# Seven block products for eight in the last two column chunks of a feed-forward input projection

## The chip, the cores and the metric

The kernel runs on one core of a Trainium2 chip. The metric is the device time of one execution in microseconds (us), the median of several. Five engines work side by side, each through its own list of instructions in order: TensorE (PE) multiplies, VectorE (DVE), ScalarE (ACT) and GpSimd (POOL) do elementwise work, SyncE (SP) issues the DMA transfers. Semaphores tie them together.

## The reference

Two layers of a decoder trunk on 256 tokens of width 1024, in float32: a feed-forward block, a mixer (gated DeltaNet and a causal convolution, merged by gates), and a second feed-forward block. There are four feed-forward blocks in all:

```python
def swiglu_ffn(h, w_in, w_out):
    gate, up = jnp.split(h @ w_in, 2, axis=-1)
    return (jax.nn.silu(gate) * up) @ w_out
...
    f = swiglu_ffn(rmsnorm(x, ffn1_norm_pre[i]), ffn1_w_in[i], ffn1_w_out[i])
    x = x + 0.5 * rmsnorm(f, ffn1_norm_post[i])
```

`w_in` is 1024 x 5632, `w_out` 2816 x 1024. The kernel scales by the norm's factor after the product, at the gate.

## The kernel before

**Numbers.** Every float32 operand is split in two: a high part, which ACT makes by a cast to PE's float32 form (`whi`, `xt[:, 0]`), and a low part, the rest, which DVE or POOL makes by a subtraction (`wlo`, `xt[:, 1]`). One product is then three matmuls (`mm3`, lines 588 to 591): high by high, high by low, low by high.

**Feed-forward stage** (`ffn`, line 694 on). The input projection (`proj_in`) goes through 11 column chunks of 512 columns (256 of the gate, 256 of the up part). A chunk has four weight tiles of 128 x 1024 (512 KB), each two 128-row pieces of the inner dimension. For both blocks of 128 tokens (`tb` 0 and 1) a weight tile serves 2 x 3 matmuls of 128 x 512, so 12 in all, and a chunk is 48 matmuls for each token block. In the last three stages the first two chunks are done for token block 0 first, while token block 1 is still being normalized. A chunk and token block fill one PSUM bank of four (`ps_mm`, tag `mm`). `ev` gates it: ACT takes Silu of one half, DVE multiplies the other (`ag`). `fin` turns the result by DVE transposes and a round trip through device memory (`way`), and splits it into high and low parts (`act`), the low part on POOL. The output projection (`proj_out`) then goes through 22 weight tiles; its four accumulators (two token blocks, two column halves) are again four `mm` banks. It takes two tiles for token block 0, both halves, then the same two for token block 1.

**Weights.** `Stream` loads the weight tiles in the order of use. A tile arrives in one of four buffers (`raw`), is cast into one of eight `whi` tiles and subtracted into one of eight `wlo` tiles (the ring, `RING = 8`). A `raw` buffer is free when its low part is made, a ring tile when PE has used it. When PE is done with a tile, the next one's load, cast and subtraction are put into the program, and a list scheduler that knows the instructions' dependencies and priorities places them in the engines' queues; PE's order is the written one. Only in the mixers are they put off by a count of matmul groups (`lanes`, `DELAY`, `in_step`), and DVE's and POOL's orders kept as written (`in_order`), with ACT's instructions held behind PE's.

## Time and profile before

| | |
|---|---|
| median of 3 runs | 1352.1 us (1351.65 to 1353.6) |
| profiled execution, span from first to last instruction | 1349.7 us |
| busy, PE / DVE / ACT / POOL | 1327.1 / 933.8 / 732.3 / 445.5 us |
| high-low products of the input projections and mixers, 128 x 512 | 2048 and 1024 matmuls |
| same, output projections | 704 and 352 |
| DMA | 273.76 MB, mean 203 GB/s |

The profiled execution's own time is told by its span only; the median of the runs lies 2.4 us above it, 0.2%. A row such as `L144 PE MATMUL mm<-whi,xt ... x2048 | 647.6, 391` reads: line 144 issued 2048 matmuls that wrote `mm` from `whi` and `xt`, busy for 647.6 us together, 391 ns from start to end of one. Matmuls overlap, so their pace is read from the starts in the timeline. The number after the second bar is the idle time ahead of the group on its engine, and what ended it.

### The profile page before, as it was taken

Reading aid. Unit: us, or ns where it says so; the run is one execution under the profiler, and the core shown is the slowest. Engines: PE = TensorE matmul, PEld = TensorE weight load, DVE = VectorE, ACT = ScalarE, POOL = GpSimd, SP = SyncE. Lnnn points to the kernel's source line nnn. Section 1 sums busy time; section 2 is a strip of 40 time slices with the busy share of each in tenths; the row PEclk is TensorE's granted clock in tenths of the full one; section 3 lists DMA queues with packets and bytes.
Section 4 is the critical chain, followed back from the end, with each engine's and each line's share of the span. In section 5 each row is a group of like instructions: output and inputs, shape, how many; then the busy total and the mean of one; then the engine's idle time right before and its main releaser. Section 6 shows DMA issues by size and latency. Waiting matters only on the chain.

```text
span 1349.7 us, 20220 instructions
## 1 busy us (share of the span) xinstructions
PE 1327.1 (98%) x7259; PEld 1128.0 (84%) x7259; DVE 933.8 (69%) x1594; ACT 732.3 (54%) x1175; POOL 445.5 (33%) x374
## 2 busy tenths in 40 slices
PE   9999999999999999999999999999999999999998
PEld 7888889997787888888888888899977878888886
DVE  6676455999966776665576654579999666766553
ACT  7545447675555545544455543577656564555541
POOL 0111017798744201111011120277986431011110
PEclk9999999999999999999999999999999999999999
DMA  8878746562634666776468775465545446477861
GB/s 274 287 239 260 249 156 210 166 211 96 206 110 153 225 218 222 276 249 221 155 219 280 265 235 186 146 231 172 173 138 183 143 139 234 154 261 247 273 212 39
DMA packets 115652, 273.76 MB, mean 203 GB/s; under 512 B 24768, under 2 KB 48352, under 8 KB 115552
## 3 DMA queue, kind: packets, MB, share of 16 engines
q1 hardware_dynamic: 115264, 272.40, 61.5%
q8 instruction: 57, 0.93, 0.3%
q14 instruction: 43, 0.35, 0.1%
q10 hardware_dynamic: 288, 0.07, 0.0%
HBM read 256.68 MB, written 15.75 MB: 202 GB/s over the span
## 4 chain that ended last, share of the span: by engine, by line
PE 81%; DVE 11%; ACT 3%; DMA 2%; issue 1%; POOL 1%; DVEq 0%; POOLq 0%; SPq 0%; ACTq 0%
PE mm L144 75%; DVE cacc L124 4%; PE gd L144 3%; DVE c L124 3%; DVE wlo L124 2%; PE tr L150 2%; DMA raw<-mw 2%; ACT whi L171 1%; DVE at L124 1%; ACT dt L171 1%; ACT sg L171 0%; DMA raw<-w2i 0%; DVE ssk L124 0%; DVE qk L124 0%; POOL rk L124 0%
## 5 line engine op out<-in xcount | busy, mean ns | idle before, releaser
L144 PE MATMUL mm<-whi,xt 128*128 128x512 f32 (+1 forms) x2048 | 647.6, 391 | 3.0 <-ACT qT L171 2.2
L171 ACT CAST whi<-raw 128x1024 fp32r<-128x1024 f32 (+2 forms) x448 | 458.8, 1035 | 316.8 <-PE mm L144 173.8
L124 DVE TENSOR_TENSOR wlo<-raw,whi 128x1024 fp32r<-128x1024 f32 (+2 forms) x342 | 427.2, 1264 | 190.0 <-ACT whi L171 183.5
L144 PEld LDWEIGHTS mm<-whi,xt 128*128 128x128 f32 x2048 | 382.3, 188 | 82.3 <-ACT qT L171 3.0
L144 PE MATMUL mm<-wlo,xt 128*128 128x512 f32 (+1 forms) x1024 | 396.4, 387 | 0.1
L124 POOL TENSOR_TENSOR wlo<-raw,whi 128x1024 fp32r<-128x1024 f32 (+1 forms) x106 | 250.5, 2379 | 142.5 <-ACT whi L171 140.0
L144 PEld LDWEIGHTS mm<-wlo,xt 128*128 128x128 f32 x1024 | 192.6, 188 | 37.6 <-DVE wlo L124 1.3
L144 PE MATMUL mm<-whi,act 128*128 128x512 f32 x704 | 218.3, 390 | 0.0
L124 POOL TENSOR_TENSOR act<-way,act 128x512 fp32r<-128x512 f32 x44 | 79.1, 1798 | 396.1 <-ACT act L171 385.9
L124 DVE SCALAR_TENSOR_TENSOR cacc<-hT,pc,cacc 128x254 f32<-128x254 f32 (+28 forms) x464 | 179.5, 472 | 0.2
L144 PE MATMUL mm<-xt,whi 128*128 128x256 f32 x960 | 175.5, 285 | 0.8 <-ACT qT L171 0.6
L144 PEld LDWEIGHTS mm<-whi,act 128*128 128x128 f32 x704 | 132.2, 188 | 27.4
L144 PEld LDWEIGHTS mm<-xt,whi 128*128 128x128 f32 x960 | 149.4, 192 | 1.9 <-ACT qT L171 0.9
L144 PE MATMUL mm<-wlo,act 128*128 128x512 f32 x352 | 137.0, 389 | 0.0
L144 PE MATMUL mm<-xt,wlo 128*128 128x256 f32 x480 | 135.9, 283 | 0.0
L171 ACT ACTIVATE ag<-mm,rstd 128x256 f32<-128x256 f32 x88 | 41.7, 474 | 100.0 <-PE mm L144 80.5
L144 PEld LDWEIGHTS mm<-xt,wlo 128*128 128x128 f32 x480 | 92.0, 192 | 0.0
L124 DVE SCALAR_TENSOR_TENSOR ag<-mm,rstd,ag 128x256 f32<-128x256 f32 x88 | 42.3, 481 | 58.7 <-ACT ag L171 58.4
L144 PEld LDWEIGHTS mm<-wlo,act 128*128 128x128 f32 x352 | 66.1, 188 | 13.6
L124 POOL TENSOR_TENSOR rpost<-ss,exp 128x1 f32<-128x1 f32 x12 | 6.5, 538 | 193.8 <-DVE ss L124 193.8
L171 ACT ACTIVATE jk<-mm 128x512 f32<-128x512 f32 x24 | 14.3, 598 | 60.4 <-PE mm L144 60.4
L124 DVE SCALAR_TENSOR_TENSOR c<-mm,pc,c 128x255 f32<-128x255 f32 (+2 forms) x108 | 43.7, 478 | 2.6 <-ACT c L171 2.6
(187 smaller groups left out, 1148.3 us busy)
## 6 DMA issues: line engine op xcount, KB each, us to landing
raw<-mw SPq DMA_DIRECT2D x168, 512.0 KB, 3.8
raw<-w2i SPq DMA_DIRECT2D x88, 512.0 KB, 4.8
raw<-w1i SPq DMA_DIRECT2D x84, 512.0 KB, 4.9
raw<-w1o SPq DMA_DIRECT2D x44, 512.0 KB, 4.7
raw<-w2o SPq DMA_DIRECT2D x44, 512.0 KB, 4.3
way<-way SPq DMA_DIRECT2D x176, 64.0 KB, 1.8
way<-way SPq DMA_DIRECT2D x44, 256.0 KB, 4.8
wbc<-feat SPq DMA_DIRECT2D x13, 512.0 KB, 4.9
```

Of the source, the lines that this page charges most:

```text
L124: r = op(out, *a, **k)
L144: r = self.eng.matmul(o, w, x, **k)
L150: r = self.eng.transpose(*a)
L171: r = op(*a, **k)
```

## The change

Chunks 9 and 10 of every feed-forward input projection (`UNITS = 4*((9,),)`) become one unit. Write X for the activations in 2 x 2 blocks (token block, half of the inner dimension) and W for the two chunks' weights in 2 x 2 blocks (half of the inner dimension, chunk). Instead of eight block products (two token blocks by two chunks by two halves of the inner dimension) there are seven, with four sums of X blocks and four of W blocks as operands, by Winograd's form of Strassen's scheme: `11`, `t1` = 12 - 11, `t2` = 22 - `t1`, `21`, `t3` = `t2` - 11, `22`, `t4` = 21 - `t2`. Each product is 12 matmuls: two weight tiles, each used by six matmuls.

- The X sums (`early`) are made on DVE near the stage's start, split by ACT and DVE, and stay in SBUF.
- The weight blocks 11 and 21 of the unit are kept in slots of their own (`held`), 12 and 22 use the `raw` buffers. DVE makes `t1`, `t2`, `t4` in PSUM banks (`sum`), `t3` in place of block 11; each in two halves of 512 columns. They are then split as other weights are.
- The seven products fill three PSUM banks, here q, r and s. q collects products 1, 3, 5 and 7, with copies taken between (`s1`, `s2`), r products 2 and 6 (copy `s5`), s product 4. Three of the four gates first add such a copy; the last one, after product 7, gates q as it stands.
- From the stage's start to the end of the input projection the loads, casts, sums and low parts of all weights, 120 tiles ahead, are put into the program by a planner (`plan`, `bring`, `best`, `issue`, `pump`): it keeps clocks for PE, DVE, ACT and POOL, and takes on each engine the job that can start first, by due time. DVE, POOL and ACT keep that written order (`in_order`, now on ACT as well). Leaving it (`plan(None)`) first forces the jobs of every tile that the ring holds, and then `lanes.flush()` the steps that are left, the last gate's product among them.
- The gates are steps with a delay (`"gate": (0, 1)`); the activations' low parts move from POOL to DVE; chunks 0 and 1, and 9 and 10, take the `way` round trip together; the numbers of `DELAY["ffn"]` change.

```diff
+UNITS = 4*((9,),)
+
+FORMS = ("11", "t1", "t2", "21", "t3", "22", "t4")
+
+SUMS = {"t1": ("12", "11"), "t2": ("22", "t1"), "t3": ("t2", "11"), "t4": ("21", "t2")}
+
+NEEDS = {"t1": (), "t2": (("t1", "low"),), "t3": (("t2", "summed"), ("11", "low")), "t4": (("t2", "low"), ("t3", "summed"))}
+
+USERS = {"12": (("t1", "summed"),), "22": (("22", "low"), ("t2", "summed")), "11": (("t3", "low"),), "21": (("21", "low"), ("t4", "summed"))}
...
     def __init__(self, eng, pe):
-        self.eng, self.pe, self.tc = eng, pe, None
+        self.eng, self.pe, self.tc, self.at = eng, pe, None, 0.0
+        self.chain, self.before = False, None
+
+    def in_order(self, tc):
+        self.tc, self.chain, self.before = tc, tc is not None, None
...
+                ins = getattr(r, "ins", r)
+                if self.chain:
+                    if self.before is not None:
+                        behind(self.tc, ins, self.before)
+                    self.before = ins
+                behind(self.tc, ins, self.pe.last)
...
+def unit_pieces(src, key, new):
+
+    raws = {(b, j): Raw(src(int(b[0]) - 1, int(b[1]) - 1, j), key(b, j)) for b in ("11", "12", "22", "21") for j in range(2)}
+    ps = {}
+    for j in range(2):
+        banks = Banks(lambda k, j=j: new(j and k))
+        at = {"t1": banks, "t2": banks, "t4": banks, "t3": raws["11", j]}
+        p = {f: Piece(at[f] if f in at else raws[f, j], f, 1.36) for f in FORMS}
+        for f in FORMS:
+            ps[f, j] = p[f]
+            p[f].group = list(raws.values())
+            if f in SUMS:
+                p[f].ins = [banks if b[0] == "t" else raws[b, j] for b in SUMS[f]]
+                p[f].needs = [(p[g], did) for g, did in NEEDS[f]]
+                p[f].parts = [slice(0, 512), slice(512, D)]
+        for b, users in USERS.items():
+            raws[b, j].users = [(p[f], did) for f, did in users]
+    return [ps[f, j] for f in FORMS for j in range(2)]
...
+    def plan(self, lanes):
+        if lanes is not None:
+            self.planned, self.lanes, lanes.stream, self.begun = True, lanes, self, self.pe.at
+            self.raws = []
+            for p in self.pieces[self.nload:self.nload + 120]:
+                for raw in p.group:
+                    if raw not in self.raws:
+                        raw.first = p.n
+                        self.raws.append(raw)
+            self.out = []
+        else:
+            for p in self.pieces[self.taken:self.nload]:
+                self.force(p)
+            self.planned, self.lanes.stream, self.lanes = False, None, None
...
+    def bring(self, now):
+        while self.raws:
+            raw = self.raws[0]
+            self.out = [r for r in self.out if not r.free(now)]
+            if raw.first > self.taken + RING + CFG["far"]:
+                break
+            if sum(r.key == raw.key for r in self.out) >= (4 if raw.key is None else 1):
+                break
+            if self.fetch > now + CFG["depth"]:
+                break
+            self.raws.pop(0)
+            raw.tile = self.fresh() if raw.key is None else self.held(raw.key)
+            self.nc.sync.dma_start(raw.tile[:, :raw.src.shape[-1]], raw.src)
+            self.fetch = max(self.fetch, now) + 1.9
+            raw.landed = self.fetch + CFG["land"]
+            self.out.append(raw)
...
+    def issue(self, eng, t, p, kind):
+        eng.at = t
+        if self.shared(p, kind):
+            self.lock = t + (2.25 if eng is self.gp else 1.08)
+        n = D if p.form else p.raw.src.shape[-1]
+        for c in p.parts if p.form else [slice(0, n)]:
+            if kind == "sum":
+                a, b = (r.part(c) for r in p.ins)
+                with prio(self.tc, "w"):
+                    eng.tensor_tensor(p.raw.part(c), a, b, op=ALU.subtract)
+            elif kind == "high":
+                self.to_high(p, c)
+            else:
+                self.to_low(p, c, eng)
+        setattr(p, {"sum": "summed"}.get(kind, kind), eng.at)
...
+    def force(self, p):
+        until = self.pe.at
+        while p.low is None:
+            until += 0.5
+            if until > self.pe.at + 100:
+                raise RuntimeError(f"stuck {p.n} {p.form}")
+            self.bring(until)
+            self.pump(until)
...
+        if first and early:
+            early()
         for c in range(len(chunks)):
+            if c in units:
+                unit(c)
+            if c in units or c - 1 in units:
+                continue
+            if c == 1 and not first and early:
+                lanes.finish(due[1])
+                early()
...
         def ev(c, tb, ps):
-            a = tokt("ag", [P, 2, 256])
-            S.activation(a[:, 0, :], ps[:, 0:256], AF.Silu, scale=xt[tb][1])
-            V.scalar_tensor_tensor(a[:, 1, :], ps[:, 256:512], xt[tb][1], a[:, 0, :], op0=ALU.mult, op1=ALU.mult)
-            gated[c, tb] = a
-
-
-
-        def fin(c):
-            act.append(slot(c, [P, 2, 2, 2, P], F32R, name="act"))
 
             def steps():
-                way = slot(11 + c % 4, [P, 2, 512], name="way")
-                out4 = way[:, 0].rearrange("p (j k b t) -> p k b j t", j=4, k=2, b=2)
-                for tb in range(2):
-                    a = gated.pop((c, tb))
-                    with prio(tc, "turn"):
-                        V.transpose(out4[:, :, tb], a[:, 1, :].rearrange("p (k j c) -> p k j c", k=2, j=4))
-                turned = dram.tile([4, 32, 4, P], F32, name=f"way{l}{c}")
+                a = gated[c, tb] = tokt("ag", [P, 2, 256])
+                with prio(tc, "ev"):
+                    S.activation(a[:, 0, :], ps[:, 0:256], AF.Silu, scale=xt[tb][1])
+                yield
+                with prio(tc, "ev"):
+                    V.scalar_tensor_tensor(a[:, 1, :], ps[:, 256:512], xt[tb][1], a[:, 0, :], op0=ALU.mult, op1=ALU.mult)
+            job = lanes.add("gate", steps())
+            if st.planned:
+                lanes.step(job)
+            else:
+                lanes.finish(job)
...
+        def fin(*cs):
+            for c in cs:
+                act[c] = slot(c, [P, 2, 2, 2, P], F32R, name="act")
+
+            def steps():
...
+                        S.copy(hi, src)
+                        V.tensor_tensor(lo, src, hi.bitcast(F32), op=ALU.subtract)
...
+            def steps():
+                p21, p11, p12 = ps_tr(), ps_tr(), ps_tr()
+                whole(p21, 1, 0)
+                whole(a[:, 0], 1, 1)
+                V.tensor_tensor(a[:, 1], p21, a[:, 0], op=ALU.add)
+                high(1, a[:, 1])
+                yield
+                whole(p11, 0, 0)
+                V.tensor_tensor(b[:, 0], a[:, 1], p11, op=ALU.subtract)
+                high(2, b[:, 0])
+                low(1, a[:, 1])
+                yield
+                V.tensor_tensor(b[:, 1], a[:, 0], b[:, 0], op=ALU.subtract)
+                high(3, b[:, 1])
+                low(2, b[:, 0])
+                yield
+                whole(p12, 0, 1)
+                V.tensor_tensor(a[:, 0], p12, b[:, 0], op=ALU.subtract)
+                high(4, a[:, 0])
+                low(3, b[:, 1])
+                yield
+                low(4, a[:, 0])
...
+        def unit(c):
+            lanes.finish(sums["job"])
+
+            def product(ps, f, start):
+                for j in range(2):
+                    w = st.peek(0)
+                    for k in range(2):
+                        kt = 2 * j + k
+                        ks = slice(512 * k, 512 * k + 512)
+                        mm3(ps, f[:, 0, kt, :], f[:, 1, kt, :], w[0][:, ks], w[1][:, ks], start and kt == 0, kt == 3,
+                            skip_group_check=True)
+                        lanes.tick()
+                    st.done()
...
+            q, r = ps_mm(), ps_mm()
+            s1, s5 = (work.tile([P, 512], F32, name="sm", tag=f"state{i}", bufs=1) for i in range(2))
+            s2 = slot(14, [P, 512], name="s2")
+            product(q, blk[0, 0], True)
+            kept(q, s1)
+            product(r, sums[1], True)
+            kept(r, s5)
+            product(q, sums[2], False)
+            kept(q, s2)
+            s = ps_mm()
+            product(s, blk[0, 1], True)
+            gate(c, 0, s, s1)
+            product(q, sums[3], False)
+            gate(c + 1, 1, q, s5)
+            product(r, sums[4], False)
+            gate(c + 1, 0, r, s2)
+            product(q, blk[1, 1], False)
+            gate(c, 1, q)
+            fin(c, c + 1)
...
+        proj_in(xt, [(512, 2)] * 11, ev, fin_one, first, units=units, unit=unit, early=early)
+        st.plan(None)
+        lanes.flush()
+        for eng in (V, W, S):
+            eng.in_order(None)
```

What this makes of the engines' lists, at three places of the first stage; the other three have the same rows with other numbers.

DVE, around the last gates of the input projection. Before (`ag_1229` and `ag_1232` gate chunk 10's two token blocks, `wlo` are low parts of output weights):

```order
L124 TENSOR_TENSOR wlo_1187<-raw_1185,whi_1186 128x1024
L124 SCALAR_TENSOR_TENSOR ag_1229<-mm_1144,rstd0_98,ag_1229 128x256
L124 STREAM_TRANSPOSE way_1251<-ag_1229 128x2x4x32
L124 SCALAR_TENSOR_TENSOR ag_1232<-mm_1145,rstd1_99,ag_1232 128x256
L124 STREAM_TRANSPOSE way_1251<-ag_1232 128x2x4x32
L124 TENSOR_TENSOR wlo_1205<-raw_1203,whi_1204 128x1024
```

and now, from the gate on the sixth product (r is `mm_1095`) to the one on the seventh (q is `mm_1094`):

```order
L134 TENSOR_TENSOR ag_1256<-mm_1095,s2_1098 128x512
L134 TENSOR_TENSOR wlo_1220<-raw_1182,whi_1219 128x1024
L134 SCALAR_TENSOR_TENSOR ag_1256<-ag_1256,rstd0_98 128x256
L134 TENSOR_TENSOR act_1093<-way_1116,act_1093 128x512
L134 TENSOR_TENSOR wlo_1233<-raw_1201,whi_1232 128x1024
L134 TENSOR_TENSOR wlo_1247<-raw_1224,whi_1246 128x1024
L134 TENSOR_TENSOR wlo_1255<-raw_1261,whi_1254 128x1024
L134 TENSOR_TENSOR wlo_1271<-raw_1280,whi_1270 128x1024
L134 TENSOR_TENSOR wlo_1283<-raw_1289,whi_1282 128x1024
L134 SCALAR_TENSOR_TENSOR ag_1284<-mm_1094,rstd1_99,ag_1284 128x256
```

The gate product `ag_1284` now stands behind five low parts in a row, those of the ring's last tiles.

PE, from the unit's last matmuls on into the output projection, the accumulators `mm_1323`, `mm_1324`, `mm_1325` (with what each waits for):

```order
L154 MATMUL mm_1323<-whi_1206,act_413 128x512
L154 MATMUL mm_1323<-wlo_1207,act_413 128x512
L154 MATMUL mm_1323<-whi_1206,act_413 128x512
L154 MATMUL mm_1324<-whi_1192,act_413 128x512 [waits DVE_49]
L154 MATMUL mm_1324<-wlo_1193,act_413 128x512
L154 MATMUL mm_1324<-whi_1192,act_413 128x512
L154 MATMUL mm_1325<-whi_1192,act_413 128x512 [waits DVE_49,Activation_49]
L154 MATMUL mm_1325<-wlo_1193,act_413 128x512
```

`mm_1325` is the 16th matmul after the unit. The counts in its two waits are reached by DVE's `ag_1284` and by the Silu ahead of it on ACT; that of `mm_1324` by the addition `ag_1256<-mm_1095`.

SP, the loads of the output weights at the unit's end:

```order
L439 DMA raw_1224<-w1o 128x1024 [waits DVE_49]
L587 DMA wbc_1632<-feat 128x1024 [waits PE_49]
L439 DMA raw_1261<-w1o 128x1024 [waits DVE_49]
L439 DMA raw_1280<-w1o 128x1024 [waits DMAHW4_49,DVE_49,Activation_49]
L439 DMA raw_1289<-w1o 128x1024 [waits DMAHW5_49,DVE_49,Activation_49]
```

`raw_1289` takes the buffer of `raw_1201`: its wait on DVE is reached by `wlo_1233<-raw_1201`.

## The prediction

> **What bounds the kernel now.** I read the page first: TensorE (PE) is busy for nearly the whole span, and its clock is granted in full. The median of the runs, 1352.1 us, lies 2.4 us above this span, so sums made against the span carry over to the median unchanged.

> ```profile
> span 1349.7 us, 20220 instructions
> PE 1327.1 (98%) x7259; PEld 1128.0 (84%) x7259; DVE 933.8 (69%) x1594; ACT 732.3 (54%) x1175; POOL 445.5 (33%) x374
> PEclk9999999999999999999999999999999999999999
> ```

> Busy does not yet mean that PE sets the end, so I next asked for PE's waits (us in total, times, longest): first the row of the longest in all,

> ```profile
> PE tr L150 <- ACT cf L171: 3.4, 2, 1.7
> ```

> then all rows of the first feed-forward stage, 0 to 170 us:

> ```profile
> PE mm L144 <- DVE idle L124: 1.3, 1, 1.3
> PE mm L144 <- ACT xt L171: 0.5, 1, 0.5
> ```

> After its start PE waits for nobody in a feed-forward stage. A product taken away there is therefore worth its full pace, and a new wait costs its full length. The pace is in PE's timeline where the input projection ends and the output projection begins:

> ```profile
> 126.27 0.39 PE L144 MATMUL mm<-wlo,xt 128*128 128x512 f32 x1
> 126.50 0.62 PE L144 MATMUL mm<-whi,xt 128*128 128x512 f32 x2
> 126.95 0.39 PE L144 MATMUL mm<-wlo,xt 128*128 128x512 f32 x1
> ...
> 127.86 0.39 PE L144 MATMUL mm<-whi,xt 128*128 128x512 f32 x1
> 128.09 0.39 PE L144 MATMUL mm<-whi,act 128*128 128x512 f32 x1
> ```

> Three matmuls take 126.95 - 126.27 = 0.68 us, so one takes 0.227 us; the 0.39 of a row is its latency, and the next one overlaps it.

> **What the change removes.** Two chunks hold 8 block products of 12 matmuls, 96; now there are 7, 84 matmuls. Twelve fewer at 0.227 us are 2.72 us a stage, and **10.9 us** for the four stages. The two mixers keep their order on every engine, so nothing else is saved on PE.

> **What it adds on the vector engines.** Four groups by form price it (busy us in all, mean ns of one),

> ```profile
> L171 ACT CAST whi<-raw 128x1024 fp32r<-128x1024 f32 x432 | 449.0, 1049 | 310.3 <-PE mm L144 170.9 <-DMA raw<-mw 55.0 <-DMA raw<-w1i 27.3
> L124 POOL TENSOR_TENSOR wlo<-raw,whi 128x1024 fp32r<-128x1024 f32 x100 | 242.4, 2440 | 128.7 <-ACT whi L171 126.2 <-DVE cacc L124 1.7 <-PE tr L150 0.2
> L171 ACT CAST act<-way 128x512 fp32r<-128x512 f32 x44 | 27.1, 616 | 2.7 <-DMA way<-way 2.7
> L124 DVE TENSOR_TENSOR xt<-tr,xt 128x512 fp32r<-128x512 f32 x20 | 13.8, 688 | 10.4 <-ACT xt L171 10.2
> ```

> then pieces of VectorE's (DVE's) timeline (start, us),

> ```profile
> 15.88 4.69 DVE L124 TENSOR_TENSOR wlo<-raw,whi 128x512 fp32r<-128x512 f32 x5
> ...
> 128.79 0.48 DVE L124 SCALAR_TENSOR_TENSOR ag<-mm,rstd,ag 128x256 f32<-128x256 f32 x1 [0.32 <-ACT ag L171]
> 129.31 0.45 DVE L124 STREAM_TRANSPOSE way<-ag 128x256 f32<-128x256 f32 x1
> 129.73 2.36 DVE L124 TENSOR_TENSOR wlo<-raw,whi 128x1024 fp32r<-128x1024 f32 x2
> 133.45 1.23 DVE L124 TENSOR_TENSOR wlo<-raw,whi 128x1024 fp32r<-128x1024 f32 x1 [1.36 <-ACT whi L171]
> ```

> and the load of three chunk-long windows (PE, weight loads, DVE, ACT, POOL busy us):

> ```profile
> 98.00:109.00 11.00, 11.00 (x50) 9.13 (x49) 7.16 (x9) 5.43 (x9) 2.42 (x2) 1.00 0.88 283
> 109.00:120.00 11.00, 11.00 (x50) 9.09 (x50) 8.02 (x9) 6.36 (x9) 2.10 (x2) 1.00 0.82 246
> 120.00:131.00 11.00, 11.00 (x50) 9.13 (x49) 8.00 (x11) 5.49 (x8) 1.45 (x1) 1.00 0.75 241
> ```

> A low part of a full weight tile costs 1.23 us alone and 2.36 - 1.23 = 1.13 behind another. Two 512-wide halves and three full tiles in 4.69 us leave (4.69 - 3 x 1.13) / 2, near 0.6 us, for a 512-wide subtraction; one that reads PSUM takes 0.69 alone, so I use 0.6 in a queue for the sums too. A gate product costs 0.48, a ScalarE (ACT) cast 1.05.

> Per stage DVE gets 16 sum halves (9.6 us), the activations' low parts that POOL had (11 x 0.6 = 6.6), 12 operations on the activations' block sums (7.2) and six more low parts, two of the unit's on POOL. An ordinary chunk then loads DVE by 4 x 1.13 + 2 x 0.48 + 2 x 0.45 + 0.6 = 7.0 of its 10.9 us, no more than the 7.2 to 8.0 of the windows, so these chunks cost nothing: PE's margin there is the ring of eight weight tiles, 8 x 2.72 = 22 us. In the unit a tile lasts PE six matmuls, 1.36 us, and the ring covers 11 us. Call PE's start of the unit time 0. The tile tightest in DVE's order is the second of the seventh product: its low part is read at 13 x 1.36 + 0.23 = 17.9 us, and DVE, working in its order from 8.9 us (below), has it at 8.9 + 0.6 + 1.2 + 1.2 + 1.13 + 0.6 + 0.5 + 0.48 + 1.2 = 15.8 (an activation low part, the seventh product's first low part, a sum, an output weight's low part, an addition, ACT's turn in between, a gate product, the low part itself). So I cost the products' own operands at nothing, with 2.1 us of cover; were it gone, the price is what exceeds it, four times over.

> **What it adds on PE's path: the last gate.** Here the order matters. DVE's old order gates chunk 10 at once; the new one puts five low parts of output weights ahead of the last gate (ag_1284), because leaving the planned mode first forces all eight tiles of the ring. PE needs that gate soon: the four accumulators of the output projection take the four PSUM banks as they come free, the last (mm_1325) takes the bank of the seventh product (mm_1094), and its wait on DVE is for that gate product. It is the 16th matmul after the unit, so PE wants it at 84 x 0.227 + 15 x 0.227 = 19.04 + 3.40 = **22.44**. Before, a gate that came at once was free: ACT began 128.29 - 128.09 = 0.20 us after PE left the chunk, and DVE ended at 129.27.

> ```profile
> 128.29 0.47 ACT L171 ACTIVATE ag<-mm,rstd 128x256 f32<-128x256 f32 x1 [0.89 <-PE mm L144]
> ```

> When does DVE get there? The low part just ahead of the gate (wlo_1283) wants raw_1289. That load goes into the buffer of raw_1201, one of four, and is issued only when DVE has done wlo_1233, four rows earlier. So the chain is: wlo_1233 done, load, cast, low part, gate product.

> - *wlo_1233 done, earliest.* Four rows before it DVE adds to the sixth product, which PE ends at 6 x 2.72 = 16.3. Then 16.3 + 0.2 + add 0.6 + low 1.13 + gate 0.48 + act low 0.6 + low 1.13 = 20.5.
> - *Latest.* Tile ring: the seventh product's first cast (two halves, 1.05) waits until PE has left the fifth tile, 5 x 1.36 = 6.8; 0.2 to ACT, the cast, 0.62 for the activation cast behind it and 0.2 to DVE give 8.9. DVE's rows from there to wlo_1233 add up, at the prices above, to the 6.9 of the last paragraph, then add 0.6, low 1.13, gate 0.48, add 0.6, low 1.13, gate 0.48, act low 0.6, low 1.13, so 8.9 + 6.9 + 6.2 = 22.0. These are the rows in sequence, so I take a value near this end, 21.5.
> - *The load.* Landings bound it: of all weight loads from 400 to 470 us, in a mixer,

> ```profile
> DMA to landing us min/median/max: 3.2/4.1/5.7
> ```

> of the one issued at 137.8 us, in the output projection,

> ```profile
> DMA to landing us min/median/max: 5.5/5.5/5.5
> ```

> and, on the page, the mixers' median:

> ```profile
> raw<-mw SPq DMA_DIRECT2D x168, 512.0 KB, 3.8
> ```

> The new loads are about 2 us apart, so I take 3.8, with 3.2 and 5.5 as ends.
> - *Cast, low, gate:* 1.05 + 1.23 + 0.48 = 2.8.

> The gate is out at 21.5 + 3.8 + 2.8 = 28.1, and PE has waited 28.1 - 22.44 = **5.7 us**; ends 20.5 + 3.2 + 2.8 - 22.44 = 4.1 and 22.0 + 5.5 + 2.8 - 22.44 = 7.9. Nothing hides it: every later matmul is queued behind mm_1325, and afterwards PE is the bound again. What DVE and ACT gain meanwhile only fills a ring that was full enough. All four stages have the same rows.

> **A restart after the wait.** PE has not stood that long anywhere inside this run. The nearest rows, of PE's timeline, are the longest wait and the start of the program:

> ```profile
> 422.81 0.66 PE L150 MATMUL tr<-cst,xhat 128*128 128x128 f32 x4 [1.72 <-ACT cf L171]
> ...
> 423.54 0.39 PE L144 MATMUL mm<-wlo,ct 128*128 128x512 f32 x1
> 423.77 0.63 PE L144 MATMUL mm<-whi,ct 128*128 128x512 f32 x2
> ...
> 1.33 3.17 PE L144 MATMUL mm<-idle 128*128 128x512 bf16 x7 [1.33 <-DVE idle L124]
> ```

> After 1.72 us the pace is whole at once (0.23 us). Out of rest, seven matmuls of the same width take 3.17 us where 7 x 0.227 = 1.59 would do: 1.6 us lost, though the clock line shows full speed. A wait of 5.7 us is over three times the one that costs nothing, so I take the start's price, **1.6 us**; ends 0 and 1.6. [...]

> **The stage's start.** In the first stage some block sums sit on DVE between the low parts that feed PE just in time: 0 to two of them late, 0 to 1.2 us; I take 0.5. In the other three they follow the second token block's operands (PE's timeline, then DVE's):

> ```profile
> 506.16 0.48 PE L144 MATMUL mm<-whi,xt 128*128 128x512 f32 x1
> ```

> ```profile
> 507.06 0.69 DVE L124 TENSOR_TENSOR xt<-tr,xt 128x512 fp32r<-128x512 f32 x1
> ```

> Twelve sums, a gate and a low part from 507.7 end near 507.7 + 7.2 + 0.15 + 0.48 + 1.13 = 516.7; PE wants that tile, the third chunk's first, 48 matmuls after 506.16, at 517.0, and its low part 0.23 later. They cost nothing with 0.6 us of cover; if the casts between the sums are late, up to 1 us each.

> **Sum.** -10.9 + 4 x (5.7 + 1.6) + 0.5 = -10.9 + 29.2 + 0.5 = +18.8 us, so 1352.1 + 18.8 = **1371**.

> **Rivals.** *No slow restart:* -10.9 + 4 x 5.7 + 0.5 = +12.4, 1364.5; with the shortest wait +6, 1358. For it: the clock line never drops and 1.72 us restart whole; against it: the start. *The saving stays:* the last gate is not late, 1352.1 - 10.9 + 0.5 = 1341.7. It decides the other way as soon as the wait is under 10.9 / 4 = 2.7 us, that is, when the gate is out before 25.1. For it: PE's margin before was ample; and the accumulator might sit in another bank. Against it: with the earliest wlo_1233 the load would have to land in 25.1 - 2.8 - 20.5 = 1.8 us, and none did under 3.2. *The change doesn't gain at all on PE:* a wait of just that size, within 0.2%, about 1352. *More waits:* sums or low parts in the unit are late too, because PSUM sums at 0.69 each and two POOL low parts at 2.44 eat the 2.1 us of cover; 2.5 us a stage above the forecast give 1381.

> **Chances.** Forecast 0.45, no slow restart 0.29, more waits 0.11, the saving stays 0.10, about equal 0.05. The range from 1356 to 1381 holds the first two with the ends of the wait and half of the third. A measurement of this kernel tells some 0.2%, 2.7 us, from no change: faster 0.10, same 0.05, slower 0.85.

> **What would show it.** PE has 48 matmuls fewer and the same 0.68 us for three. Its waits have four long ones (4 to 8 us) of an output-projection matmul for DVE's gate product, each some 3.4 us after a unit; in DVE's timeline the gate stands behind low parts, the last of which waited for ACT and that for a load. The matmuls behind such a wait run at 0.45 us for some us, or at 0.23 at once. The prediction is wrong if PE passes from the unit to the output projection without that wait, or if it waits inside the unit.

## The result, and the profile after

The changed kernel took 1388.95 us, the median of four runs (1387.87 to 1391.33), against 1352.42 us for the kernel before on the same chip: a ratio of 1.0274, 95% interval 1.0259 to 1.0288. It is slower, as predicted, but by 36.5 us where 18.8 were predicted, above the top of the range (1381). The profiled execution was the longest of the four (1391.3 us), so the account of its span below runs some 2.4 us above the median.

The page of the changed kernel, its span, its busy times and TensorE's granted clock by slices:

```profile
span 1389.5 us, 20274 instructions
PE 1335.6 (96%) x7211; PEld 1130.2 (81%) x7211; DVE 1035.0 (74%) x1810; ACT 772.9 (56%) x1259; POOL 390.0 (28%) x338
PEclk9999999999999999999999989999999999999999
```

PE has the 48 matmuls fewer (7259 to 7211), yet its busy time has grown. Its waits (us in total, times, longest) show the first reason:

```profile
PE mm L154 <- DVE ag L134: 29.2, 8, 6.9
...
PE mm L154 <- DVE wlo L134: 2.7, 3, 2.3
```

No row of either kind stood there before. The eight waits for DVE's gate tile (`ag`) are of two kinds. The page's groups part them by what PE multiplies (busy us, mean ns of one, idle time ahead of the group and what ended most of it):

```profile
L154 PE MATMUL mm<-whi,xt 128*128 128x512 f32 (+1 forms) x1888 | 603.4, 393 | 10.9 <-DVE ag L134 6.2
...
L154 PE MATMUL mm<-whi,act 128*128 128x512 f32 x704 | 225.8, 400 | 23.0 <-DVE ag L134 23.0
```

The products with `act` belong to the output projection: four waits for the last gate, 23.0 us, 5.75 each, where 5.7 was forecast. The 6.2 us ahead of products with `xt` stand inside the units, where nothing was forecast. In PE's timeline of the first stage (start, us, count, and in brackets the wait ahead and what ended it) both are to be seen, and what comes behind the long one:

```profile
129.54 0.50 PE L154 MATMUL mm<-whi,xt 128*128 128x512 f32 x1 [1.56 <-DVE ag L134]
...
142.93 0.76 PE L154 MATMUL mm<-whi,act 128*128 128x512 f32 x1 [6.93 <-DVE ag L134]
143.49 0.63 PE L154 MATMUL mm<-wlo,act 128*128 128x512 f32 x1
143.92 1.05 PE L154 MATMUL mm<-whi,act 128*128 128x512 f32 x2
144.77 0.63 PE L154 MATMUL mm<-wlo,act 128*128 128x512 f32 x1
```

The wait at 129.54 is for the bank q. Product 7 writes on into it, and DVE's addition after product 5, which reads it, stood behind a gate product and two halves of a low part and was done at 128.81 + 0.68 = 129.49. VectorE's timeline:

```profile
127.21 0.48 DVE L134 SCALAR_TENSOR_TENSOR ag<-ag,rstd 128x256 f32<-128x256 f32 x1 [0.58 <-ACT ag L189]
127.61 1.28 DVE L134 TENSOR_TENSOR wlo<-sum,whi 128x512 fp32r<-128x512 f32 x2
128.81 0.68 DVE L134 TENSOR_TENSOR ag<-mm,sm 128x512 f32<-128x512 f32 x1
```

Behind the long wait three matmuls take 144.77 - 143.49 = 1.28 us instead of 0.68. That is the clock. The record of the granted clock has eight half-speed stretches before the program's end, where the profiled execution of the kernel before has none. A table of these eight windows (length, then busy us of PE, weight loads, DVE, ACT, POOL, then PE's granted clock, the DMA share and GB/s) gives their price; three rows and the sum:

```profile
45.70:49.10 3.40, 3.40 (x9) 2.65 (x8) 3.19 (x6) 0.00 (x0) 0.00 (x0) 0.50 0.94 279
141.30:148.10 6.80, 5.17 (x12) 4.13 (x13) 4.04 (x7) 1.96 (x2) 0.00 (x0) 0.50 0.91 272
...
346.10:349.50 3.40, 3.40 (x18) 3.40 (x17) 3.40 (x9) 1.85 (x6) 3.17 (x5) 0.51 0.00 0
...
sum 40.80, PE 32.85 PEld 27.55 DVE 29.30 ACT 13.27 POOL 6.33; mean PE 4.11 PEld 3.44 DVE 3.66 ACT 1.66 POOL 0.79
```

PE worked for 32.85 us at half speed, so 16.4 us were lost: 9.6 behind the four last gates, 1.7 behind a wait in a unit, 1.7 at the first stage's start, 3.4 in the two mixers. Their number varies from one execution to the next: the mean clock of the change's four executions is 0.984 to 0.988, so that some 44 to 33 us of each ran at half speed, the program's end included. The account of the span (+39.8): -10.9 for the matmuls, +23.0 and +6.2 for the gate tile, +2.7 for low parts, +16.4 for the clock, which leaves 2.4 us in small waits that I did not assign.

VectorE's timeline shows that the chain of the last gate is the one the prediction described:

```profile
138.55 1.23 DVE L134 TENSOR_TENSOR wlo<-raw,whi 128x1024 fp32r<-128x1024 f32 x1 [1.00 <-ACT whi L189]
141.16 1.23 DVE L134 TENSOR_TENSOR wlo<-raw,whi 128x1024 fp32r<-128x1024 f32 x1 [1.39 <-ACT whi L189]
142.30 0.48 DVE L134 SCALAR_TENSOR_TENSOR ag<-mm,rstd,ag 128x256 f32<-128x256 f32 x1
```

and ScalarE's timeline has the cast that it hung on, which waited for a load:

```profile
140.09 1.04 ACT L189 CAST whi<-raw 128x1024 fp32r<-128x1024 f32 x1 [1.57 <-DMA raw<-w1o]
```

### The profile page after: what moved, and what is told of

It is laid out like the page before. It is cut to its first block, busy times and chain, and to the rows that moved or that the text cites. A ratio compares the mean times of both kernels' runs of the same rounds, so it can differ in the third digit from the quotient of the medians.

```text
span 1389.5 us, 20274 instructions
## 1 busy us (share of the span) xinstructions
PE 1335.6 (96%) x7211; PEld 1130.2 (81%) x7211; DVE 1035.0 (74%) x1810; ACT 772.9 (56%) x1259; POOL 390.0 (28%) x338
## 4 chain that ended last, share of the span: by engine, by line
PE 59%; DVE 17%; DMA 8%; ACT 6%; issue 5%; POOL 4%; SPq 0%; DVEq 0%; POOLq 0%; ACTq 0%
PE mm L154 54%; DVE wlo L134 6%; PE gd L154 3%; DMA raw<-w1i 3%; DVE cacc L134 3%; ACT whi L189 3%; DVE c L134 3%; POOL wlo L134 2%; DMA raw<-mw 2%; PE tr L160 1%; DMA raw<-w1o 1%; DMA raw<-w2o 1%; DMA raw<-w2i 1%; DVE sum L134 1%; DVE ag L134 1%
## 5 line engine op out<-in xcount | busy, mean ns | idle before, releaser
L189 ACT CAST whi<-raw 128x1024 fp32r<-128x1024 f32 (+1 forms) x424 | 434.0, 1035 | 342.0 <-PE mm L154 134.6
L154 PE MATMUL mm<-whi,xt 128*128 128x512 f32 (+1 forms) x1888 | 603.4, 393 | 10.9 <-DVE ag L134 6.2
L134 DVE TENSOR_TENSOR wlo<-raw,whi 128x1024 fp32r<-128x1024 f32 (+2 forms) x314 | 377.5, 1217 | 163.3 <-ACT whi L189 158.8
L154 PEld LDWEIGHTS mm<-whi,xt 128*128 128x128 f32 x1888 | 353.7, 189 | 88.0 <-DVE ag L134 8.7
L154 PE MATMUL mm<-wlo,xt 128*128 128x512 f32 (+1 forms) x944 | 366.6, 388 | 2.7 <-DVE wlo L134 2.6
L134 POOL TENSOR_TENSOR wlo<-raw,whi 128x1024 fp32r<-128x1024 f32 (+1 forms) x110 | 260.9, 2386 | 167.9 <-ACT whi L189 165.6
L154 PEld LDWEIGHTS mm<-wlo,xt 128*128 128x128 f32 x944 | 178.3, 189 | 37.8 <-DVE wlo L134 4.6
L134 POOL TENSOR_TENSOR wlo<-held,whi 128x1024 fp32r<-128x1024 f32 x4 | 9.7, 2413 | 329.2 <-ACT whi L189 246.5
L134 DVE TENSOR_TENSOR act<-way,act 128x512 fp32r<-128x512 f32 x44 | 33.1, 760 | 14.5 <-ACT act L189 14.4
L189 ACT CAST whi<-sum 128x512 fp32r<-128x512 f32 x48 | 26.0, 589 | 30.8 <-DVE sum L134 21.8
## 6 DMA issues: line engine op xcount, KB each, us to landing
raw<-mw SPq DMA_DIRECT2D x168, 512.0 KB, 3.5
raw<-w2i SPq DMA_DIRECT2D x80, 512.0 KB, 5.3
raw<-w1i SPq DMA_DIRECT2D x76, 512.0 KB, 5.3
raw<-w1o SPq DMA_DIRECT2D x44, 512.0 KB, 4.4
raw<-w2o SPq DMA_DIRECT2D x44, 512.0 KB, 4.2
wbc<-feat SPq DMA_DIRECT2D x13, 512.0 KB, 4.4
```

The source lines that it names most:

```text
L134: r = op(out, *a, **k)
L154: r = self.eng.matmul(o, w, x, **k)
L189: r = op(out, *a, **k)
```

## The experiments

All kernels here compute the whole reference. Each ratio is to the kernel before, on the same chip.

**1. The last gate ahead of the forced parts.** One edit in `ffn`, just before the planned mode is left:

```diff
+        for job in [j for j in lanes.jobs if j[1] == "gate"]:
+            lanes.finish(job)
         st.plan(None)
```

> The changed kernel with one edit: the step of the last gate is put into the program before the planner is left, so its DVE product stands ahead of the five low parts of output weights instead of behind them. Theory A (the gate queued behind low parts that wait for loads, and the slow restart after it): PE's four waits for it, 23.0 us together, go, and with them the half-speed stretches behind them, some 4 x 2.4 us; 1389 - 23 - 10 = 1356 us, within 3. Rival B (the vector engines are simply too busy in the unit): the wait moves to the low parts and the time stays above 1380.

Measured: 1352.57 us, ratio 1.000 (0.9991 to 1.0010), so 36.4 us less than the change and 0.4 under A's range. The four waits ahead of `mm<-whi,act` are gone:

```profile
L154 PE MATMUL mm<-whi,act 128*128 128x512 f32 x704 | 218.5, 390 | 0.0
```

This is more than their 23.0 us. The half-speed stretches behind them went as well, and both mixers' too, so only two were left in the profiled execution (at 46.3 and at 616.3 us, the second within a wait of 2.88 us for product 7). Where DVE puts the last gate is thus the main cause. What is left, 5.9 us of waits for gates (nearly all of it product 7), 2.8 for low parts and 4 to 5 for the clock, more than uses up the saving of 10.9 in this execution, the longest of ten; by the median it uses it up.

**2. The planner alone.** No unit, no sums: eleven chunks by eight products, the planner in charge.

```diff
-UNITS = 4*((9,),)
+UNITS = 4*((),)
...
```

> The changed kernel without any unit: all 11 chunks with eight block products, no sums of activations or weights, but the planner, the kept orders, the delayed gates and the activations' low parts on DVE as in the change. Theory A (the loss is the unit's: two waits for gates, and the activations' sums and kept blocks at the first stage's start): no wait of PE for a gate, 1352 to 1357 us. Rival C (the planned order loses by itself): 1370 us or more, with waits of PE in ordinary chunks.

Measured: 1358.91 us, ratio 1.0051 (1.0035 to 1.0067): slower, and above theory A's 1352 to 1357. A had expected no wait for a gate; there are four, as the groups show:

```profile
L154 PE MATMUL mm<-whi,act 128*128 128x512 f32 x704 | 219.1, 390 | 6.3 <-DVE ag L134 6.3
```

The way out of the planned mode delays the last gate even after ordinary chunks (1.2 to 2.6 us a stage); with the unit ahead of it that was 5.75.

**3. Three mends at once.** The gate first; a ScalarE copy of q after product 5, so that product 7 waits for the copy and not for DVE's addition; and the loads of the kept blocks held back behind PE's progress.

```diff
+            s6 = slot(15, [P, 512], name="s6")
+            kept(q, s6)
-            gate(c + 1, 1, q, s5)
+            gate(c + 1, 1, s6, s5)
...
+            if raw.key is not None:
+                behind(self.tc, getattr(r, "ins", r), self.pe.last)
```

> The changed kernel with three edits: the last gate first (as in the run of that name), a copy of the fifth product's sum by ACT so that the seventh product waits for ACT's copy and not for DVE's addition, and the loads of the kept weight blocks held back behind PE's work instead of going out at the program's start. Theory A: the gate's 23.0 us, the seventh products' 6.2, the start's 2.3 and the half-speed stretches behind all of them go; what is left is the 10.9 us saved: 1352.4 - 10.9 = 1341.5, up to 1346 us. If the start's stall is the planner's order and not the early loads, some 4 us more than with it gone, and the wait for a low part at 45 us stays. Rival B: above 1365 us.

Measured: 1360.01 us, ratio 1.0057 (1.0042 to 1.0072), worse than the first mend alone, and between A and B. The wait for product 7 only changed hands, and grew: with 9.8 us for it, 2.6 for low parts and 6.6 for four half-speed stretches (half of 13.18 us of PE's busy time) the span should be 19.0 - 10.9 = 8.1 us longer, and it is 8.8. PE's waits:

```profile
PE mm L154 <- ACT s L189: 9.8, 4, 3.4
```

and ScalarE's timeline ahead of the one of 3.39 us in the first stage:

```profile
130.16 1.98 ACT L189 CAST whi<-raw 128x1024 fp32r<-128x1024 f32 x2
132.04 0.57 ACT L189 COPY s<-mm 128x512 f32<-128x512 f32 x1
```

The copy stands behind two casts in ScalarE's fixed order, as the addition had stood behind a low part in DVE's. Both readers of q were late; the fault is that PE needs q back at once. The stall at the first stage's start stayed (1.87 us), so the early loads of the kept blocks are not its cause.

**4. TensorE kept busy in the wait.** The change as it is, with 20 matmuls into a spare bank ahead of the 16th matmul of the output projection, each stage.

```diff
+                if warm and kt == 0 and tb == 1 and hf == 1:
+                    warm.clear()
+                    spare = ps_tr([P, 512])
+                    for _ in range(20):
+                        T.matmul(spare, idle[:, 0:P], idle[:, P:640], start=True, stop=True)
```

> The changed kernel with 20 matmuls of 128 x 512 in bfloat16 that nobody reads, put ahead of the matmul that waits for the last gate, in each stage: some 4.3 us of PE's wait filled with work. Theory A (half the pace after a wait is the clock after standing idle): the wait for the gate keeps its end, the half-speed stretches behind the four gates go, and the time falls by about 4 x 2.4 to some 1379 us. Rival D (the slow matmuls behind the wait have another cause, such as late operands): same pace as without, 1389 us or more by what the added matmuls overrun.

Measured: 1378.21 us, ratio 1.0199 (1.0180 to 1.0217): PE does more, and the kernel is 10.7 us faster than the change. In the profiled execution the granted clock has no half-speed stretch left before the program's end. PE's timeline, at the same place:

```profile
136.07 4.26 PE L154 MATMUL tr<-idle 128*128 128x512 bf16 x19
142.29 0.47 PE L154 MATMUL mm<-whi,act 128*128 128x512 f32 x1 [1.96 <-DVE ag L134]
142.60 0.39 PE L154 MATMUL mm<-wlo,act 128*128 128x512 f32 x1
142.83 0.63 PE L154 MATMUL mm<-whi,act 128*128 128x512 f32 x2
143.29 0.39 PE L154 MATMUL mm<-wlo,act 128*128 128x512 f32 x1
```

(One of the 20 has no record.) The gate comes only 0.6 us earlier than in the change, but three matmuls take 143.29 - 142.60 = 0.69 us. So the slow restart is the price of standing still, and not of the operands. The stretches far from the spare matmuls, at the first stage's start, at product 7 and in the mixers, did not come up either in this execution. The other three have a mean clock of 0.993 to 0.997, so there some did, where is not on record; the last section returns to these.

**5. A bank of its own for product 7.** On top of the first mend, which now finishes the gates with an addition too: a copy of q is taken after product 5, but the addition reads q as before; product 7 fills a fresh bank, and the last gate adds the copy.

```diff
             gate(c + 1, 1, q, s5)
+            s6 = slot(15, [P, 512], name="s6")
+            kept(q, s6)
...
-            product(q, blk[1, 1], False)
-            gate(c, 1, q)
+            t = ps_mm()
+            product(t, blk[1, 1], True)
+            gate(c, 1, t, s6)
```

> Left in place: the last gate issued ahead of the forced low parts. New: after product 5 ScalarE copies q to SBUF, product 7 accumulates in a PSUM bank of its own, and the last gate adds the copy to it. Theory A (product 7 waited only because DVE's addition still read the bank that it writes): the 5.9 us of waits of the run with the gate first go, and with them the half-speed stretch at 616 us of 6.8 us, which cost about 3.4 us: 1352.6 - 5.9 - 3.4 = 1343, range 1341 to 1346, and the stall of 2.3 us at 45.5 us stays. Rival B (the gate, one addition longer, only moves the wait to the first matmuls of the output projection, which take over the banks): no wait at product 7 but as much at the sixteenth matmul behind it: 1349 to 1355. Rival C (the extra copy on ScalarE delays the unit's casts, and PE waits for whi or wlo there): 1350 or more, with new rows of waits for whi.

Measured: 1348.79 us, ratio 0.9976 (0.9965 to 0.9988). The profiled execution was the longest of twelve (1354.8 us; the shortest took 1345.6), so its rows show a bad case. No wait is left at product 7 in any unit, but part of it came back behind the unit, as rival B had it: PE's timeline has these two for the last gate, now one addition longer, besides one of 0.54 us in the last stage.

```profile
135.43 0.50 PE L154 MATMUL mm<-whi,act 128*128 128x512 f32 x1 [0.65 <-DVE ag L134]
...
802.53 0.50 PE L154 MATMUL mm<-whi,act 128*128 128x512 f32 x1 [2.10 <-DVE ag L134]
```

By the ratios the gain on the first mend is 0.0024, 3.2 us. The waits account for 5.9 - 3.7 = 2.2 of it; a half-speed stretch of 3.4 us in place of one of 6.8 is of the size of the rest. The median lies between A and B.

**6. The planner later in the last three stages.** On top of experiment 5. The text expected this of the first stage; the condition that the edit uses holds in the other three, where the first two chunks run for one token block ahead. So the run tells about these, and leaves the first stage as it was.

```diff
-        if first and early:
-            early()
         for c in range(len(chunks)):
+            if c == 4 and first and early:
+                early()
```

> The same as the run with a bank of its own, and in the first feed-forward stage alone the planner takes over ahead of column chunk 4 and not ahead of chunk 0. Theory A (the stall at 45.5 us comes from the planner's clocks and fixed order in the first stage, which run ahead of engines that are still late from the start of the program; by chunk 4 they have caught up): the 2.3 us of wait and the half-speed stretch of 3.4 us behind it (about 1.7 us lost) go: 4 us below the run with a bank of its own, about 1339. Rival B (the stall belongs to the hand-over itself): it appears again near 75 to 80 us, and the time is that of the run with a bank of its own within 1 us. Rival C (eight chunk loads more at the old pace leave too little time for the sums ahead of the unit): new waits for xs or wlo in the first unit, 1345 or more.

Measured: 1346.84 us, ratio 0.9968 (0.9956 to 0.9980). The intervals of this run and the last overlap; a gain of 1 to 2 us by the later start is possible and not shown. The stall of the first stage stands unchanged, as it must:

```profile
45.99 0.50 PE L154 MATMUL mm<-wlo,xt 128*128 128x512 f32 x1 [2.33 <-DVE wlo L134]
```

**7. The planner alone, with the gate first.** Experiment 2 with the edit of experiment 1.

> All eleven column chunks by eight products, no unit and no sums, the planner in charge, and the last gates issued ahead of the forced low parts. Theory A (the 6.3 us of waits for the last gates that the planner alone showed come from their place behind the forced parts): 1358.9 - 6.3 = 1352.6, range 1351.5 to 1354, the same as before the change. Rival B (they come from the planner's order of gates at every chunk): 1357 to 1360, and the waits for ag stay.

Measured: 1350.97 us, ratio 0.9992 (0.9983 to 1.0002). This is 0.5 us under A's range. No wait for `ag` is left, one of 0.23 us for a low part, and no half-speed stretch before the program's end. By itself the planner costs nothing that these runs can tell; its exit did. The stall at the first stage's start is missing too, so it needs the unit or its sums.

**8. The sums of X later in the first stage.** On top of experiment 6.

```diff
             sums["job"] = lanes.add("forms", steps())
+            sums["job"][0] += 0 if first else 48
```

> The run with a bank of its own and the planner from column chunk 4 in the three later stages; in the first stage the ten vector operations of the weight-independent sums are put 48 beats (three column chunks) later, the planner still from chunk 1. Theory A (the sums, on VectorE from 22 to 31 us, push the low parts back there, the loads behind those come late, and the low part for 45.99 us ends up behind two gates and four transposes; the planner alone, without sums, showed no such wait): the wait of 2.33 us and the half-speed stretch of 3.4 us behind it go: 1346.8 - 4 = 1343, range 1341.5 to 1344.5. Rival B (the planner's hand-over at chunk 1 is the cause, with or without sums): the stall stays, 1346 to 1348. Rival C (the sums, moved, push back the low parts of a later chunk just the same): a wait for wlo of 1 to 3 us near 70 to 90 us, 1345 to 1348.

Measured: 1344.85 us, ratio 0.9942 (0.9930 to 0.9954), the fastest of all, and faster than the kernel before by 7 to 8 us. The stall and its half-speed stretch are gone (A), and the time is 0.35 us above A's range. VectorE's timeline in the change, where the low part PE waits for stands behind gates and transposes:

```profile
36.96 0.69 DVE L134 TENSOR_TENSOR xs<-xa,xs 128x512 fp32r<-128x512 f32 x1 [1.60 <-ACT xs L189]
41.32 0.88 DVE L134 SCALAR_TENSOR_TENSOR ag<-mm,rstd,ag 128x256 f32<-128x256 f32 x2 [3.66 <-ACT ag L189]
42.11 1.41 DVE L134 STREAM_TRANSPOSE way<-ag 128x256 f32<-128x256 f32 x4
43.45 4.59 DVE L134 TENSOR_TENSOR wlo<-raw,whi 128x1024 fp32r<-128x1024 f32 x4
```

and with the sums moved:

```profile
36.97 0.87 DVE L134 SCALAR_TENSOR_TENSOR ag<-mm,rstd,ag 128x256 f32<-128x256 f32 x2
37.76 1.22 DVE L134 TENSOR_TENSOR wlo<-raw,whi 128x1024 fp32r<-128x1024 f32 x1
38.89 1.42 DVE L134 STREAM_TRANSPOSE way<-ag 128x256 f32<-128x256 f32 x4
40.23 2.32 DVE L134 TENSOR_TENSOR wlo<-raw,whi 128x1024 fp32r<-128x1024 f32 x2
```

Two smaller waits have come, one in the first unit (1.20 us for a low part) and one behind it (1.49 for the last gate), and one half-speed stretch of 3.4 us in a mixer. The account closes: -10.9 + 1.7 (`ag`) + 1.4 (`wlo`) + 1.7 (clock) = -6.1, and the span is 1349.7 - 1343.7 = 6.0 shorter.

**9. Planner and sums later in the first stage.** On top of experiment 6, `early` is called in the first stage ahead of chunk 4 and not 1.

> The same start, but in the first stage planner and sums both begin ahead of column chunk 4 and not 1. Theory A (the start is sensitive since loads and VectorE are still late there; by chunk 4 the raw buffers are full): no stall, 1343, range 1341.5 to 1344.5, the same as with the sums alone moved. Rival B (the hand-over itself disturbs the order wherever it is): a wait for wlo of 1 to 3 us within two chunks of 57 us, 1345 to 1348.

Measured: 1352.15 us, ratio 0.9997 (0.9985 to 1.0009): a miss for A. The early stall is gone, but another came later, for a gate and not for a low part. PE's timeline,

```profile
88.24 0.50 PE L154 MATMUL mm<-whi,xt 128*128 128x512 f32 x1 [2.96 <-DVE ag L134]
```

VectorE's,

```profile
84.82 0.69 DVE L134 TENSOR_TENSOR act<-way,act 128x512 fp32r<-128x512 f32 x1 [11.20 <-ACT act L189]
85.43 2.35 DVE L134 TENSOR_TENSOR wlo<-raw,whi 128x1024 fp32r<-128x1024 f32 x2
87.70 0.87 DVE L134 SCALAR_TENSOR_TENSOR ag<-mm,rstd,ag 128x256 f32<-128x256 f32 x2
```

and ScalarE's:

```profile
84.17 0.62 ACT L189 CAST act<-way 128x512 fp32r<-128x512 f32 x1 [10.47 <-DMA way<-way]
```

In the fixed order a cast that waited 10.47 us for the activations' round trip stood ahead of weight casts and gates, so VectorE was idle for 11.20 us with work behind it. That is not rival B's stall either: B put a wait for a low part within two chunks of 57 us, that is by 79 us. Why the round trip was late there is not shown. Three half-speed stretches (one behind this wait, two in mixers) add to it.

## Why the prediction failed on size, point by point

- **The saving, -10.9: right.** 48 matmuls fewer, and 0.68 us for three wherever the clock is full. Experiment 8's account closes with it.
- **"Nothing hides it", the last gate at 5.7 us a stage: right.** Measured 5.75 (6.93, 5.07, 5.20, 5.79), the gate's product behind low parts, the last of them behind a load. Experiment 1 took the wait away by the order alone. That the size came out to 0.05 us is luck: counted from the unit's start the gates were done at 28.6 to 32.7 us, 30.5 on average, and not at 28.1, since DVE was done with wlo_1233 and its like at 22.6 to 26.2 and not at 21.5; but PE, held up by product 7, came for them at 23.5 to 27.5, 24.7 on average, and not at 22.44. The two errors of some 2.3 us cancel.
- **"I take the start's price, 1.6 us", for the restart: mechanism right, size wrong.** By PE's busy time at half clock it was 2.6, 2.6, 2.1 and 2.4 us, 9.6 in all for 6.4. The start of the program was a poor ruler. The clock line shows full speed there, but the clock's record begins only at 4.87 us, when the seven slow matmuls are over (4.50); in experiment 4 it begins at 9.14, and matmuls just before that start 0.43 us apart. Here a stretch lasts 6.8 us, of which 1.6 to 2.6 us fall into the wait and the rest is PE's slow time. The 1.6 us were thus too small: here a last gate's stretch was two lengths of 3.4 us. The rival without a slow restart (0.29) falls with experiment 4.
- **"So I cost the products' own operands at nothing": the step that failed.** Operands were indeed nearly in time. What was left out is that product 7 writes on into q, which DVE reads for the addition after product 5, and that PE must wait for this read. Price 6.2 us (1.56, 0.77, 3.11 and 0.77), and 1.7 for the clock behind one of the four; experiment 5, with a bank of its own, took these waits away. The last section of the prediction named a wait inside the unit as its own refutation.
- **"In the first stage ... I take 0.5": too small.** The wait was 2.33 us and the clock behind it cost 1.7. I priced the sums by VectorE's busy time and not by their effect on the order: with them the kept order put two gates and four transposes, which come when PE has finished a chunk, ahead of a low part that PE needed first. Experiment 8 against 6 shows that the sums' place is the cause; that it works through the raw buffers, as its expectation had it, is only argued.
- **"The two mixers keep their order on every engine, so nothing else is saved": not the whole of it.** The order stayed, but two half-speed stretches came there, 3.4 us. That the change brought them is not shown: 13 of the 54 executions of the kernel before that were timed beside the experiments have a mean clock of 0.997, some 8 us at half speed, of which the program's end takes 1.2 to 4.1 us in the kept traces.

The terms then read: 18.8 forecast, + 0.2 last gate, + 3.2 restart, + 7.9 product 7, + 3.9 start (2.7 + 1.7 - 0.5), + 3.4 mixers = 37.4 for 39.8 measured on the span. The rival "more waits" (0.11) was nearest to it in kind, and its 1381 was too low since it, too, did not have the clock behind such waits; and it looked for late operands, not for a bank that is still being read.

## What to carry to other kernels

Where a program has a written order on an engine, ask of each step that is forced at a boundary what it stands ahead of: here one loop, put ahead of the forced steps, was worth 36 us. When accumulations share a bank, list its readers as well as its writers; here product 7, which went on in a bank, waited 0.77 to 3.11 us a stage for DVE's read of it; another reader did not help (9.8 us of waits for ScalarE's copy), and another bank did. And price a wait of TensorE with the slow work behind it, not by its length alone: in the change that work cost 1.7 us behind each wait of 2.33 and 3.11 us, 2.1 to 2.6 us behind each of those of 5.07 to 6.93 us, and none behind those of 0.77 and 1.56 us.

## What the runs showed of the hardware

```profile
137.90:141.30 3.40, 0.00 (x0) 0.00 (x0) 1.36 (x2) 1.66 (x2) 0.00 (x0) 0.99 0.78 293
813.70:817.10 3.40, 0.37 (x2) 0.33 (x3) 2.83 (x6) 2.77 (x4) 0.00 (x0) 1.00 0.93 258
```

The slot ahead need not be wholly idle: in the change PE was busy for 1.08 us of the one at 42.27 us, and half speed followed. The wait of 2.33 us at the first stage's start was enough there and in experiments 1, 5 and 6, and one of 1.87 us in experiment 3, while the kernel before has 1.72 us without it, and in experiment 4 a wait of 2.66 us for product 7 went by without it too. So in these traces the length of a wait alone does not decide; its place on the grid does, too. The kept traces tell, since the grid lies differently in each. In experiment 5 a wait of 2.10 us for the last gate (802.53 us) fell into one slot, and half speed followed:

```profile
799.80:803.20 3.40, 1.30 (x6) 0.77 (x5) 2.11 (x5) 2.04 (x5) 0.00 (x0) 1.00 0.76 257
803.20:806.60 3.40, 3.40 (x10) 2.63 (x9) 3.40 (x4) 1.81 (x2) 0.00 (x0) 0.51 0.28 64
```

In experiment 3 the grid cut a wait of 2.82 us for product 7 (621.86 us) in two, and the clock stayed full:

```profile
617.10:620.50 3.40, 1.94 (x9) 1.28 (x7) 2.82 (x6) 2.26 (x5) 0.00 (x0) 1.00 0.78 231
620.50:623.90 3.40, 2.04 (x9) 1.71 (x10) 2.72 (x5) 2.64 (x4) 0.00 (x0) 1.00 0.91 312
```

Of the feed-forward stages' slots at full speed in the traces of the kernel before, the change and experiments 1, 3, 4 and 5, the program's start and end apart, 13 have PE busy for 1.54 us or less, and 12 of these were followed by half speed (the other, with 1.48 us, is in experiment 4, beside the spare matmuls, one of which has no record); none with 1.57 us or more was. The mixers do not divide as cleanly: in the change, two slots there with 1.63 and 1.69 us of PE were followed by half speed, two others with 1.69 us were not; what tips them is open. The one at 346.1 follows these rows of PE's timeline,

```profile
343.94 1.15 PE L160 MATMUL tr<-cst,vT 128*128 128x128 f32 x6 [1.46 <-ACT vT L189]
...
345.89 1.00 PE L160 MATMUL tr<-cst,qT 128*128 128x128 f32 x4 [0.36 <-ACT vr L189]
```

in which PE only transposes, with waits between that the kernel before has too.

**VectorE beside GpSimd.** In the first unit of the change an activation's low part took 2.31 us on VectorE, where it takes 0.68 in experiment 8. VectorE's row and GpSimd's:

```profile
120.20 2.31 DVE L134 TENSOR_TENSOR act<-way,act 128x512 fp32r<-128x512 f32 x1 [0.51 <-ACT act L189]
```

```profile
118.75 3.21 POOL L134 TENSOR_TENSOR wlo<-raw,whi 128x1024 fp32r<-128x1024 f32 x1 [6.06 <-ACT whi L189]
```

Both ran at once, from 120.20 to 121.96; GpSimd's took 2.40 in the unit's other tile. In the second and fourth stage the same low part took 1.51 us (617.80 and 1303.63 us) beside GpSimd's of 2.41 us, and ran together with it for 0.96 us. So VectorE's took 0.83 us more for 0.96 us of overlap, and 1.63 more for 1.76. In experiment 8 GpSimd's part was over before (114.72 to 117.43). No run was made for this alone.
